# 1/rms of the feed-forward blocks as a row from a matrix of ones, in place of a column that is transposed

## The chip, the core and the metric

The kernel runs on one core of a Trainium2 chip. The metric is the time of one execution on the device in microseconds (us). TensorE is PE (its weight loads are PEld), VectorE is DVE, ScalarE is ACT, GpSimd is POOL, and SP is the engine that starts the loads. A matrix product takes its stationary operand (the weights) and a moving operand, and writes to PSUM, which POOL cannot read.

## What is computed

The reference is a decoder trunk of two layers on 256 tokens of 1024 features. Only the outline matters here:

```
for l in range(DEPTH):                       # DEPTH = 2
    x = x + 0.5 * _swiglu(_rmsnorm(x, ffn1_norm[l]), ffn1_w_gate[l], ffn1_w_up[l], ffn1_w_down[l])
    h = _rmsnorm(x, mix_norm[l])
    ...                                      # attention of three kinds on h @ w_in[l], then w_out[l]
    x = x + 0.5 * _swiglu(_rmsnorm(x, ffn2_norm[l]), ffn2_w_gate[l], ffn2_w_up[l], ffn2_w_down[l])
return _rmsnorm(x, final_norm)

def _rmsnorm(x, g):
    y = x32 * lax.rsqrt(jnp.mean(x32 * x32, axis=-1, keepdims=True) + RMS_EPS)
    return (y * g).astype(x.dtype)
def _swiglu(x, w_gate, w_up, w_down):
    return (jax.nn.silu(x @ w_gate) * (x @ w_up)) @ w_down
```

There are four feed-forward blocks (1024 to 2816 and back), two in each layer, with the attention between them.

## The kernel before

**Layout.** x is held transposed: `x[k]` has 128 features on the partitions and the 256 tokens on the free axis, for k from 0 to 7. The sum of squares of a token therefore runs over partitions. 1/rms of a token is needed as a *row*: the same 256 numbers on every partition (`rrow`), which is multiplied to the product x·W after the fact.

**Precision.** Every weight chunk (128x1024 numbers, `raw`) is split into a high part (`whi`, ACT, L157) and the rest (`wlo`, DVE, L158). The splits run three chunks ahead of PE (`SPLIT_AHEAD`). The operands `xx` hold x in the same two parts. `mm2` multiplies `whi` with both parts of x (512 columns) and `wlo` with the high part (256 columns); this pair of matmuls is the unit of PE's work.

**A feed-forward block** (`ffn`). `products(i, h)` runs eight pairs with one weight chunk; chunks (i, 0) and (i, 1) fill two PSUM banks, gate and up, of the column tile i, for i from 0 to 21. The banks come from two rings of four, and tile i+3 or so takes the banks of tile i. Behind them, for each i: `a` (DVE, L304, twice, with a copy `b` by ACT) adds the halves and frees the bank, `t` (DVE, L346) multiplies gate by the row, `s` (ACT) is silu, `sr` (POOL, L350) multiplies by the row again, `h` (DVE, L352) multiplies by up, and two more operations split h. Then the eight column tiles of the down projection follow.

**1/rms before.** The squares are summed over k on ACT and POOL (`ss`, `fold`). In products(2, 0), after the first pair (n = 0), `column` multiplies the sums by a column of ones: two matmuls with one moving column each (`pss`, L267 reads them) give mean squares with tokens on the partitions, as 128x2. DVE scales them (`ms`, L267), POOL raises them to the power -1/2 (`rcol`, L269). After pair n = 9, PE transposes the broadcast column (`prow`, L218) and DVE copies it out of PSUM (`rrow`, L281). The attention uses the same functions at other places, and `rcol` itself as well.

**What sets the order.** The engines' queues are in order; the scheduler of the framework places the instructions from the order of the code and its own estimates. PE's order is written down (`in_order`). The splits are put behind the instruction in `urgent`.

Of the kernel before, what the change touches and what calls it, by code (L numbers as in the profile page):

```python
# [10 lines left out]
F32 = mybir.dt.float32  # L11
F32R = mybir.dt.float32r
AF = mybir.ActivationFunctionType
OP = mybir.AluOpType

P = 128
D = 1024
T = 256
# [11 lines left out]
EPS = 1e-6  # L30
# [6 lines left out]
CH = DK * P  # L37
RAW, SPLIT_AHEAD = 5, 3
WARM = 12
AT = (0, 9)  # L40

FIRST = ((0, 1), (1, 4))

# [35 lines left out]
def tile_trunk(ctx, tc, xT, gains, kvg, sinks, table, onehot, wgu, wdn, winv, wins, wkv, wout, out):  # L79
    nc = tc.nc  # L80

    const = ctx.enter_context(tc.tile_pool(name="const", bufs=1))
    wpool = ctx.enter_context(tc.tile_pool(name="wpool", bufs=2))
    act = ctx.enter_context(tc.tile_pool(name="act", bufs=1))
    tmp = ctx.enter_context(tc.tile_pool(name="tmp", bufs=3))
# [3 lines left out]
    def bank(name, tag="mm"):  # L89
        return psum.tile([P, 512], F32, tag=tag, name=name)  # L90

    def f(ap):
        return ap.bitcast(F32)
# [33 lines left out]
    urgent = [None, None]  # L127
# [16 lines left out]
    def split(n, pieces=1, after=None):  # L144

        if n < len(chunks) and n not in parts:
            load(n)
            w = chunks[n][2]
            parts[n] = halves_of(n)
            step = w // pieces  # L150
            for c in range(0, w, step):
                split_part(n, c, c + step, after)
# [14 lines left out]
    def next_w(pieces=1, ahead=True):  # L167
        n = cursor[0]
        cursor[0] += 1
        split(n)  # L170
        if ahead:
            split(n + SPLIT_AHEAD, pieces)
        load(n + 2 * RAW - 1)
        return parts.pop(n)
# [23 lines left out]
                            fill=1.0, base=0, channel_multiplier=1)  # L198
    ones = const.tile([P, 1], F32, name="ones")
    nc.vector.memset(ones, 1.0)  # L200
    mhalf = const.tile([P, 2], F32, name="mhalf")
    nc.vector.memset(mhalf, -0.5)

# [7 lines left out]
    def in_order(ins):  # L211
        last_pe[0] = behind(ins, last_pe[0])

    def matmul(*a, **kw):
        in_order(nc.tensor.matmul(*a, **kw))  # L215

    def transpose(*a):
        in_order(nc.tensor.transpose(*a))  # L218
# [41 lines left out]
    def rms_column(sums, n):  # L260
# [8 lines left out]
        nc.gpsimd.tensor_tensor(out=col, in0=v, in1=mhalf, op=OP.pow)  # L269
        return col  # L270

    def rms_psum(col):

        p = bank("prow", "at")
        for b in range(2):
            transpose(p[:, b * P:(b + 1) * P], col[:, b:b + 1].to_broadcast([P, P]), ident)
        return p[:, :T]

    def rms_row(col):
        row = tmp.tile([P, T], F32, tag="rrow", name="rrow", bufs=2)  # L280
        urgent[1] = nc.vector.tensor_copy(row, rms_psum(col))  # L281
        return row
# [6 lines left out]
    def mm2(out, whi, wlo, both, first, last):  # L289

        matmul(out, whi, both.rearrange("p a t -> p (a t)"), start=first, stop=False)
        matmul(out[:, :T], wlo, both[:, 0, :], start=False, stop=last)

    def residual(a, b, p, scale, nxt, last=False):
        nc.vector.scalar_tensor_tensor(xs[:, a:b, :], p, scale, xs[:, a:b, :], op0=OP.mult, op1=OP.add)
        if not last:
            for k in range(a, b):
                nxt.operands(k)

    def add_halves(p, tag):  # L300
        b = tmp.tile([P, T], F32, tag=tag, name="b")
        nc.scalar.copy(b, p[:, T:])  # L302
        a = tmp.tile([P, T], F32, tag=tag, name="a")
        nc.vector.tensor_add(a, p[:, :T], b)  # L304
        return a

    def ffn(norm, nxt, last=False, first=None, between=(), at=AT):
        hs, banks, ws = [], {}, {}

        def products(i, h, start=0, stop=DK):  # L310

            if start == 0:
                ws[0] = next_w(ahead=(i, h) not in ((1, 1), (2, 0)))
                if h == 0:
                    for m in range(2):
                        banks[i, m] = bank("pgu", "at" if i % 3 == 2 else "mm")
            whi, wlo = ws[0]
            for j in range(start, stop):
                k, m = h * DK // 2 + j // 2, j % 2
                c = slice(j * P, (j + 1) * P)  # L320
                mm2(banks[i, m], whi[:, c], wlo[:, c], xx[k], k == 0, k == DK - 1)


        products(0, 0)
        products(0, 1)
        if first:
            first()
        products(1, 0)
        products(1, 1)
        for n in range(2 * DK):  # L330
            products(2, n // DK, n % DK, n % DK + 1)
            if n == at[0]:
                col = norm.column()
                for m in range(2):
                    split(cursor[0] + SPLIT_AHEAD - 2 + m)
            if n == at[1]:
                row = rms_row(col)
        for i in range(FK):
            if i in between:
                between[i]()  # L340
            if i > 2:
                products(i, 0)
                products(i, 1)
            g, u = add_halves(banks.pop((i, 0)), "A"), add_halves(banks.pop((i, 1)), "C")
            t = tmp.tile([P, T], F32, tag="A", name="t")
            nc.vector.tensor_mul(t, g, row)  # L346
            s = tmp.tile([P, T], F32, tag="B", name="s")
            nc.scalar.activation(s, t, AF.Silu)  # L348
            sr = tmp.tile([P, T], F32, tag="B", name="sr")
            nc.gpsimd.tensor_mul(sr, s, row)  # L350
            h = tmp.tile([P, T], F32, tag="h", name="h", bufs=2)
            nc.vector.tensor_mul(h, sr, u)  # L352
            hs.append(act.tile([P, 2, T], F32R, tag=("hh", "hl")[i % 2], name=f"h{i}", bufs=FK // 2))
            nc.scalar.copy(hs[i][:, 0, :], h)  # L354
            nc.vector.tensor_sub(hs[i][:, 1, :], h, f(hs[i][:, 0, :]))
        for k in range(DK):
            p = bank("pdn")
            for kk in range(FK):
                j = (k * FK + kk) % DK
                if j == 0:  # L360
                    whi, wlo = next_w()
                c = slice(j * P, (j + 1) * P)
                mm2(p, whi[:, c], wlo[:, c], hs[kk], kk == 0, kk == FK - 1)
            if last and k:
                turn(k - 1)
            nc.vector.scalar_tensor_tensor(x[k], p[:, T:], 0.5, x[k], op0=OP.mult, op1=OP.add)
            residual(k, k + 1, p[:, None, :T], 0.5, nxt, last)
            nxt.square(k, last)
            if last:
                ys[k] = tmp.tile([P, T], F32, tag="A", name="y")  # L370
                nc.scalar.activation(ys[k], x[k], AF.Copy, scale=nxt.g(k))
# [3 lines left out]
    def turn(k):  # L375

        for b in range(2):
            if k % 4 == 0:
                turned[b, k // 4] = bank("turned", ("mm", "at")[b])
            transpose(turned[b, k // 4][:, k % 4 * P:(k % 4 + 1) * P], ys[k][:, b * P:(b + 1) * P], ident)  # L380
# [334 lines left out]
    norm = Norm(0)  # L715
# [8 lines left out]
    start = norm  # L724
# [5 lines left out]
    for l in range(DEPTH):  # L730
        nxt = Norm(3 * l + 1)
        ffn(norm, nxt, first=first_squares if l == 0 else None, between={3: load_bias, 6: make_bias} if l == 0 else {})
        norm, nxt = nxt, Norm(3 * l + 2)
        mix(l, norm, nxt)
        norm, nxt = nxt, Norm(3 * l + 3)
        ffn(norm, nxt, last=l == DEPTH - 1)
        norm = nxt

    col = norm.column()
# [88 lines left out]
```

## Time and profile before

| | |
|---|---|
| median of three runs | 972.0 us (971.95 to 972.46) |
| the profiled execution | 966.4 us, span 964.6 us from the first to the last instruction |
| granted TensorE clock, mean over the span | 0.997 |
| busy: PE, DVE, ACT, POOL | 948.2, 689.9, 554.3, 180.7 us |
| pow on POOL (`rcol`), nine times | 10.0 us |

Busy time says how long an engine had an instruction in work. The durations below are from the profiled execution, whose own time is 5.6 us under the median of the runs.

### The profile page before, as it was taken

The numbers are of one execution on the slowest core, as the hardware profiler recorded it, in microseconds if no ns is written. First come the engines' busy times: TensorE is split into PE (matmuls) and PEld (weight loads), VectorE is DVE, ScalarE is ACT, GpSimd is POOL, SyncE is SP. The second block draws the span as 40 slices with busy tenths as digits, with TensorE's granted clock in tenths as the row PEclk, the third lists the DMA queues.
The fourth block names the chain that finished last, engine by engine and source line by source line (L and its number), as shares of the span: only waits on it lengthen the run. The fifth ranks groups of instructions, "written<-read, shape, count | busy, mean of one in ns | idle before, by whom it ended". The sixth has DMA issues, their size and how long they took to land.

```text
span 964.6 us, 15601 instructions
## 1 busy us (share of the span) xinstructions
PE 948.2 (98%) x5924; PEld 842.7 (87%) x5924; DVE 689.9 (72%) x1235; ACT 554.3 (57%) x1024; POOL 180.7 (19%) x156
## 2 busy tenths in 40 slices
PE   7999999999999999999999999999999999999996
PEld 6888888898899888888888888889988988888885
DVE  5787775659747888776668778666795578877552
ACT  6655554446875655554456555544487576655442
POOL 3221110121213212210022212001132042121001
PEclk9999999999999999999999999999999999999998
DMA  9688655554424565555555555555433345556511
GB/s 338 209 302 303 207 179 186 186 179 137 149 89 162 189 207 186 181 207 180 184 196 189 179 203 187 181 185 186 148 133 130 133 175 202 192 179 201 190 44 43
DMA packets 47575, 174.41 MB, mean 181 GB/s; under 512 B 3291, under 2 KB 5867, under 8 KB 47372
## 3 DMA queue, kind: packets, MB, share of 16 engines
q1 hardware_dynamic: 47212, 172.90, 51.4%
q8 instruction: 46, 0.75, 0.3%
q10 hardware_dynamic: 288, 0.52, 0.1%
q14 instruction: 29, 0.24, 0.1%
HBM read 172.34 MB, written 4.22 MB: 183 GB/s over the span
## 4 chain that ended last, share of the span: by engine, by line
PE 86%; DVE 4%; ACT 4%; issue 3%; POOL 1%; DMA 1%; SPq 0%; POOLq 0%; DVEq 0%; ACTq 0%
PE pgu L215 50%; PE pdn L215 22%; PE pwo L215 5%; PE pp L215 4%; PE pv L215 2%; ACT e L594 1%; ACT e L576 1%; DVE wlo L158 1%; POOL ss L248 1%; DVE acc L499 1%; PE po L215 1%; DVE m L498 1%; ACT whi L157 1%; DMA xs<-xT 1%; PE pt L218 1%
## 5 line engine op out<-in xcount | busy, mean ns | idle before, releaser
L215 PE MATMUL pgu<-xx,whi 128*128 128x512 f32 x1408 | 491.1, 393 | 2.4 <-DVE xx L235 1.5
L158 DVE TENSOR_TENSOR wlo<-raw,whi 128x1024 fp32r<-128x1024 f32 (+3 forms) x314 | 383.4, 1224 | 136.5 <-ACT whi L157 129.0
L157 ACT CAST whi<-raw 128x1024 fp32r<-128x1024 f32 (+2 forms) x322 | 332.7, 1034 | 244.1 <-PE pdn L215 108.1
L215 PE MATMUL pgu<-xx,wlo 128*128 128x256 f32 x1408 | 393.9, 280 | 0.2 <-DVE wlo L158 0.2
L215 PEld LDWEIGHTS pgu<-xx,whi 128*128 128x128 f32 x1408 | 263.6, 187 | 62.2 <-ACT whi L157 3.0
L215 PEld LDWEIGHTS pgu<-xx,wlo 128*128 128x128 f32 x1408 | 265.8, 189 | 0.9 <-DVE wlo L158 0.8
L215 PE MATMUL pdn<-h,whi 128*128 128x512 f32 x704 | 245.7, 394 | 0.0
L215 PE MATMUL pdn<-h,wlo 128*128 128x256 f32 x704 | 196.7, 279 | 0.0
L350 POOL TENSOR_TENSOR sr<-s,rrow 128x256 f32<-128x256 f32 x88 | 98.1, 1114 | 351.9 <-ACT s L348 351.6
L215 PEld LDWEIGHTS pdn<-h,whi 128*128 128x128 f32 x704 | 131.8, 187 | 29.6
L215 PEld LDWEIGHTS pdn<-h,wlo 128*128 128x128 f32 x704 | 132.9, 189 | 0.0
L302 ACT COPY b<-pgu 128x256 f32<-128x256 f32 x176 | 65.1, 371 | 78.8 <-PE pgu L215 78.8
L215 PE MATMUL pp<-xx,whi 128*128 128x256 f32 x480 | 90.7, 289 | 0.0
L304 DVE TENSOR_TENSOR a<-pgu,b 128x256 f32<-128x256 f32 x176 | 73.5, 419 | 23.6 <-ACT b L302 23.1
L215 PEld LDWEIGHTS pp<-xx,whi 128*128 128x128 f32 x480 | 74.2, 191 | 2.7 <-issue 1.7
L215 PE MATMUL pp<-xx,wlo 128*128 128x256 f32 x240 | 67.7, 282 | 0.0
L352 DVE TENSOR_TENSOR h<-sr,a 128x256 f32<-128x256 f32 x88 | 37.4, 425 | 29.1 <-POOL sr L350 28.7
L215 PE MATMUL pwo<-ohl,whi 128*128 128x256 f32 x256 | 47.6, 287 | 0.0
L248 POOL TENSOR_TENSOR ss<-sq 128x512 f32<-128x512 f32 x7 | 10.2, 1460 | 195.4 <-ACT sq L243 195.4
L354 ACT CAST h<-h 128x256 fp32r<-128x256 f32 x88 | 35.2, 400 | 19.0 <-DVE h L352 19.0
L215 PEld LDWEIGHTS pp<-xx,wlo 128*128 128x128 f32 x240 | 45.8, 191 | 0.0
L348 ACT ACTIVATE s<-t 128x256 f32<-128x256 f32 x88 | 37.4, 425 | 6.0 <-DVE t L346 5.5
(99 smaller groups left out, 714.4 us busy)
## 6 DMA issues: line engine op xcount, KB each, us to landing
raw<-wgu SPq DMA_DIRECT2D x86, 1024.0 KB, 5.0
raw<-wdn SPq DMA_DIRECT2D x44, 1024.0 KB, 5.0
raw<-wins SPq DMA_DIRECT2D x14, 1024.0 KB, 5.0
raw<-wout SPq DMA_DIRECT2D x8, 1024.0 KB, 4.9
raw<-winv SPq DMA_DIRECT2D x4, 776.0 KB, 4.3
w<-u SPq DMA_DIRECT2D x1, 3072.0 KB, 14.1
bias<-w SPq DMA_DIRECT2D x1, 2048.0 KB, 9.3
raw<-wgu SPq DMA_DIRECT2D x3, 512.0 KB, 8.1
```

The lines of the kernel that those rows point to most:

```text
L157: ops = (nc.scalar.copy(hi[:, a:b], raw(n, a, b)), low.tensor_sub(lo[:, a:b], raw(n, a, b), f(hi[:, a:b])))
L158: low.tensor_sub(lo[:, a:b], raw(n, a, b), f(hi[:, a:b])))
L215: in_order(nc.tensor.matmul(*a, **kw))
L218: in_order(nc.tensor.transpose(*a))
L248: nc.gpsimd.tensor_add(s, self.sums[0], sq)
L302: nc.scalar.copy(b, p[:, T:])
L304: nc.vector.tensor_add(a, p[:, :T], b)
L348: nc.scalar.activation(s, t, AF.Silu)
L350: nc.gpsimd.tensor_mul(sr, s, row)
L352: nc.vector.tensor_mul(h, sr, u)
L354: nc.scalar.copy(hs[i][:, 0, :], h)
L498: nc.vector.max(out=m8, in_=acc[:, cs])
```

## The change

In the four feed-forward blocks the sums of squares are multiplied by a 128x128 matrix of ones (`every`), which gives the sum of each token on every partition at once (`pss`, now 128x256). DVE scales it (`mrow`) and POOL raises all of it to -1/2 (`rrow`). The transposition after pair 9 and its copy are gone. The attention and the last norm keep the column.

```diff
-AT = (0, 9)
+AT = 0
...
+    every = const.tile([P, P], F32, name="every")
+    nc.vector.memset(every, 1.0)
...
+    def rms_spread(sums, n):
+
+        p = bank("pss", "at")
+        for i, s in enumerate(sums):
+            matmul(p[:, :T], every, s, start=i == 0, stop=i == len(sums) - 1)
+        v = tmp.tile([P, T], F32, tag="B", name="mrow")
+        urgent[1] = nc.vector.tensor_scalar(v, p[:, :T], 1.0 / n, EPS, op0=OP.mult, op1=OP.add)
+        row = tmp.tile([P, T], F32, tag="rrow", name="rrow", bufs=2)
+        nc.gpsimd.tensor_tensor(out=row, in0=v, in1=mhalf[:, 0:1].to_broadcast([P, T]), op=OP.pow)
+        return row
...
-            if n == at[0]:
-                col = norm.column()
+            if n == at:
+                row = rms_spread(norm.sums, D)
                 for m in range(2):
                     split(cursor[0] + SPLIT_AHEAD - 2 + m)
-            if n == at[1]:
-                row = rms_row(col)
```

On POOL, in each feed-forward block, the row of the power stands between the sum of squares and the 22 products `sr`. Before, in the second block of layer 0:

```order
L248 TENSOR_TENSOR ss<-sq 128x512
L248 TENSOR_TENSOR ss<-ss,sq 128x512 x2
L252 TENSOR_TENSOR fold<-ss 128x256
L269 TENSOR_TENSOR rcol<-ms,mhalf 128x2
L350 TENSOR_TENSOR sr<-s,rrow 128x256 x22
```

and now (the lines have moved by 2 to 13):

```order
L250 TENSOR_TENSOR ss<-sq 128x512
L250 TENSOR_TENSOR ss<-ss,sq 128x512 x2
L254 TENSOR_TENSOR fold<-ss 128x256
L282 TENSOR_TENSOR rrow<-mrow,mhalf 128x256
L361 TENSOR_TENSOR sr<-s,rrow 128x256 x22
```

Only the size of the power has changed there: 256 columns in place of 2. On DVE, the same block from the scaling of the mean squares on; the three `wlo` are the low parts of chunks (3, 0), (3, 1) and (4, 0), the first two `t` are those of the column tiles 0 and 1. Before:

```order
L267 TENSOR_SCALAR ms<-pss 128x2
L158 TENSOR_TENSOR wlo_3561<-raw_3345,whi_3560 128x1024
L158 TENSOR_TENSOR wlo_3565<-raw_3345,whi_3564 128x1024
L304 TENSOR_TENSOR a<-pgu,b 128x256
L281 COPY rrow<-prow 128x256
L158 TENSOR_TENSOR wlo_3583<-raw_3405,whi_3582 128x1024
L346 TENSOR_TENSOR t<-a,rrow 128x256
L304 TENSOR_TENSOR a<-pgu,b 128x256
L346 TENSOR_TENSOR t<-a,rrow 128x256
L158 TENSOR_TENSOR wlo_3667<-raw_3405,whi_3666 128x1024
```

and now:

```order
L280 TENSOR_SCALAR mrow<-pss 128x256
L158 TENSOR_TENSOR wlo_3556<-raw_3341,whi_3555 128x1024
L158 TENSOR_TENSOR wlo_3560<-raw_3341,whi_3559 128x1024
L357 TENSOR_TENSOR t<-a,rrow 128x256
L317 TENSOR_TENSOR a<-pgu,b 128x256
L158 TENSOR_TENSOR wlo_3578<-raw_3401,whi_3577 128x1024
L317 TENSOR_TENSOR a<-pgu,b 128x256
L363 TENSOR_TENSOR h<-sr,a 128x256
L357 TENSOR_TENSOR t<-a,rrow 128x256
L317 TENSOR_TENSOR a<-pgu,b 128x256
```

The copy is gone, and the first `t`, which reads the row, has moved ahead of the `a` of tile 1 and of the split of chunk (4, 0). The other three blocks read alike around `mrow`.

## Rows read from the trace of the kernel before

**Rows 1.** The page, part 1: busy us (share of the span) xinstructions of each engine.

```profile
PE 948.2 (98%) x5924; PEld 842.7 (87%) x5924; DVE 689.9 (72%) x1235; ACT 554.3 (57%) x1024; POOL 180.7 (19%) x156
```

**Rows 2.** Waits of PE over the span: who for whom, total us, times, longest.

```profile
PE pss L215 <- ACT sq L511: 1.8, 2, 1.0
...
PE pss L215 <- POOL fold L252: 1.2, 1, 1.2
...
PE pgu L215 <- DVE wlo L158: 0.2, 1, 0.2
```

**Rows 3.** Timeline of PE, second block of layer 0: start, us, engine, line, operation.

```profile
310.69 0.60 PE L215 MATMUL pss<-ones,fold 128*128 128x1 f32 x4
311.16 0.48 PE L215 MATMUL pgu<-xx,whi 128*128 128x512 f32 x1
...
314.42 0.38 PE L218 MATMUL prow<-ident,rcol 128*128 128x128 f32 x2
314.56 0.48 PE L215 MATMUL pgu<-xx,whi 128*128 128x512 f32 x1
...
316.74 0.39 PE L215 MATMUL pgu<-xx,whi 128*128 128x512 f32 x1
...
319.51 0.39 PE L215 MATMUL pgu<-xx,whi 128*128 128x512 f32 x1
319.74 0.28 PE L215 MATMUL pgu<-xx,wlo 128*128 128x256 f32 x1
...
322.28 0.39 PE L215 MATMUL pgu<-xx,whi 128*128 128x512 f32 x1
```

**Rows 4.** Timeline of POOL, the same block; in brackets the idle time before.

```profile
311.58 1.63 POOL L269 TENSOR_TENSOR rcol<-ms,mhalf 128x2 f32<-128x2 f32 x1 [0.94 <-DVE ms L267]
319.68 1.80 POOL L350 TENSOR_TENSOR sr<-s,rrow 128x256 f32<-128x256 f32 x2 [6.47 <-ACT s L348]
```

**Rows 5.** Timeline of DVE, the same block.

```profile
311.34 0.16 DVE L267 TENSOR_SCALAR ms<-pss 128x2 f32<-128x2 f32 x1 [0.63 <-PE pss L215]
311.42 2.36 DVE L158 TENSOR_TENSOR wlo<-raw,whi 128x1024 fp32r<-128x1024 f32 x2
313.69 0.42 DVE L304 TENSOR_TENSOR a<-pgu,b 128x256 f32<-128x256 f32 x1
314.84 0.42 DVE L281 COPY rrow<-prow 128x256 f32<-128x256 f32 x1 [0.73 <-PE prow L218]
315.18 1.22 DVE L158 TENSOR_TENSOR wlo<-raw,whi 128x1024 fp32r<-128x1024 f32 x1
316.31 0.42 DVE L346 TENSOR_TENSOR t<-a,rrow 128x256 f32<-128x256 f32 x1
```

**Rows 6.** The tile rcol: POOL's power, duration ns min/median/max, first and last start.

```profile
L269 POOL TENSOR_TENSOR rcol<-ms,mhalf x9: 699/705/1631, 23.6 to 957.9; 128x2 f32<-128x2 f32 x9
```

**Rows 7.** The tile rrow: POOL's product by the row, same columns.

```profile
L350 POOL TENSOR_TENSOR sr<-s,rrow x88: 737/1126/1557, 31.8 to 893.7; 128x256 f32<-128x256 f32 x88
```

**Rows 8.** The tile ss: POOL's sum of squares, same columns.

```profile
L248 POOL TENSOR_TENSOR ss<-sq x7: 1297/1357/1797, 14.7 to 924.6; 128x512 f32<-128x512 f32 x7
```

**Rows 9.** Timeline of all engines in the first block, POOL beside DVE.

```profile
18.80 2.24 POOL L248 TENSOR_TENSOR ss<-ss,sq 128x512 f32<-128x512 f32 x1
...
20.12 2.00 DVE L158 TENSOR_TENSOR wlo<-raw,whi 128x1024 fp32r<-128x1024 f32 x1
```

**Rows 10.** Timeline of PE in the attention: a full-precision product of 256 columns, two passes.

```profile
258.82 0.68 PE L215 MATMUL pk<-cg,wk 128*128 128x256 f32 x2
259.34 0.55 PE L215 MATMUL pk<-wk,cg 128*128 128x64 f32 x4
```

**Rows 11.** Stretches at the end: us, busy of PE, PEld, DVE, ACT, POOL, granted clock, DMA.

```profile
950.00:958.00 8.00, 6.81 (x44) 5.83 (x42) 1.01 (x3) 1.03 (x2) 0.11 (x1) 1.00 0.00 0
958.00:964.60 6.60, 0.00 (x0) 0.00 (x0) 1.41 (x2) 1.26 (x2) 0.59 (x1) 0.50 0.42 159
```

**Rows 12.** Timeline of ACT, second block of layer 0.

```profile
319.19 0.42 ACT L348 ACTIVATE s<-t 128x256 f32<-128x256 f32 x1
```

## The prediction

> **What bounds the kernel now.** I read the shares of busy time first, then what PE waited for, then the second block of layer 0 engine by engine. PE is busy for 948.2 of 964.6 us [rows 1], and its eight kinds of wait add up to 9.5 us, from 1.8 to 0.2 [rows 2]. So PE is the bound: whatever the change moves on DVE or POOL gains nothing, unless PE comes to wait for it, and then all of that wait is paid.
>
> What has to be seen in the block is how much time lies between the mean squares and the first need of what hangs on them. PE goes on at 311.16, behind `pss`, with 15 more pairs of products(2), starts products(3, 0) at 316.74 and (3, 1) at 319.51, where the first matmul with the low part stands at 319.74, and products(4, 0) at 322.28 [rows 3]; a pair takes 0.35 us. DVE has `ms` at 311.34, then the low parts of chunks (3, 0) and (3, 1), 2.36 us for both, and is through with them at 313.78 [rows 5]. So chunk (3, 1) is ready 6 us early. The power on POOL starts at 311.58 and ends at 313.21 [rows 4], and the longest of PE's waits in all, 1.8 us, is for something else [rows 2].
>
> **PE's part of the change.** Removed are the `pss` of one column, 311.16 - 310.69 = 0.47 us, and the transpositions, 314.56 - 314.42 = 0.14 us [rows 3]. Added is one full-precision product with 256 moving columns; the nearest row is `pk`, of that very shape, which takes 259.34 - 258.82 = 0.52 us [rows 10]. Together -0.1 us for each block. The wait for `fold` ahead of `pss`, 1.2 us in one block [rows 2], stays, since the place of `pss` does.
>
> **DVE's part.** `ms` (0.16 us) and the copy (0.42 us) go [rows 5]; `mrow` has 256 columns from PSUM as the copy has, so 0.42 us at the same place. Bounds: 0.16 to 0.42. DVE is 72% busy [rows 1], and the 0.2 us less are behind PE's work. The memset of the matrix of ones, once, lies ahead of all loads. These edits cost nothing as long as DVE keeps its lead. No transfer is added or moved.
>
> **The power.** This is the term that decides. The row of before shows it with 2 columns only: 699 ns at least, 705 in the median, up to 1631 [rows 6]. The long ones are those in the feed-forward blocks: the power starts at 311.58, just after a split has started on DVE at 311.42, and ends 0.6 us after that split is over (half of 2.36 us, at 312.60) [rows 4, 5]. So a split and a POOL instruction hold each other up. It goes the other way too: a split that takes 1.22 us alone [rows 5] takes 2.00 us at 20.12, when a sum on POOL runs until 21.04, and ends 1.08 us after it [rows 9].
>
> What do 256 columns cost? Two bounds:
> - From below, by the shape: a product of 256 columns takes 737 ns at least [rows 7], a sum of 512 columns 1297 [rows 8]. That is 2.2 ns for a column and 177 ns for an instruction. If the power cost 2.2 ns for a column, and the rest of its 700 ns were paid once, it would take 1.3 us.
> - From above, by the operation: of the 700 ns, 177 are those of any instruction, which leaves 523 ns for 2 columns, 261 ns for each. By that, 256 columns take 0.18 + 256 x 0.261 = 67 us. If even the 177 ns were paid by the column, 256 x 0.35 = 90 us.
>
> A rule of the Trainium skill speaks for the lower end: its page GPSIMD Engine Reference, section Performance versus the Vector engine, gives about 2.6 cycles an element for a two-input operation, measured with an add; at its clock of 1.2 GHz that is an estimate of 0.55 us for 256 columns, and by it the change would cost nothing (971.6 us, first rival). The sum and the product in this trace agree, 2.2 ns a column; the power of 2 columns, at 700 ns in place of some 181, does not.
>
> I take the upper row, 261 ns a column, because it is the only one of this operation, and the product and the sum differ from it in kind, not only in size: it spends 519 ns more than the product's line gives for 2 columns. How much of this is paid once, no row says.
>
> **What is late, then.** `mrow` ends at some 311.9 (0.26 us more than `ms`, and a longer `pss`), the first split follows and ends at about 313.0; the power then reads, and ends 0.61 us later if it has 2 columns. So the row is there at R = 313.6 + 254 c, where c is the price of a column. The second split stands behind the first on DVE and, by what the rows show of splits and POOL, waits for the power; it ends at R + 1.2. PE needs it at 319.74 - 0.14 + 0.05, about 319.65. Nothing else PE could do is ahead of it. So PE waits R + 1.2 - 319.65 us, if that is above zero: from c = 19 ns on. With c = 261 ns, R = 380.0 and PE waits 61.6 us. Should the split slip in ahead of the power, the next in line is products(4), due at 322.1: the second bank of it is freed by the `a` that stands behind the first `h`, and this behind `t`, `s` and `sr`, 2.5 to 3 us after R (0.42 + 0.42 + 0.74 to 1.13 + 0.42 + 0.42) [rows 5, 7, 12]; PE would wait 60 to 61 us all the same.
>
> Behind the wait two things are to be paid. DVE has the work of two column tiles to make good, and chunk (4, 1) stands behind six operations of 256 columns (0.42 us each) and its own split of 1.22 us [rows 5], 3.7 us in all, against 2.8 us of PE's next eight pairs: about 1 us. And PE's clock: at the end, PE runs nothing from 958.0 on, and the granted clock is 0.50, half of 2.4 GHz, where it was 1.00 [rows 11]. A wait of 60 us will end at the half clock. No row shows for how long; bounds 0 to 4 us lost, I take 1.5. Together 2.5 us.
>
> **The sum.** For each block 61.6 + 2.5 - 0.1 = 64.0 us; the four blocks are built alike, so 256 us. The profiled execution's own time is 966.4 us (span 964.6), which makes 1222; the median of the runs is 5.6 us above it, and so is my forecast: 1228 us.
>
> **The rivals.**
> 1. *The power is hidden: not slower.* POOL pays its 519 ns once and then 2 to 19 ns a column. With 2.2 ns, R = 314.2, the second split ends at 315.4, 4 us ahead of PE. What is left is 4 x -0.1 = -0.4 us: 971.6 us. For it: the lines of sum and product [rows 7, 8]. Against it: the 700 ns for two columns [rows 6]. It decides below 19 ns a column; above, each 10 ns cost 4 x 2.54 = 10 us. A gain above 0.2% (2 us, about what a measurement of this kernel can tell from no change) could only come from order, since 9.5 us of waits is all that PE has [rows 2].
> 2. *POOL overlaps its columns.* Two columns may be too few to show a rate: a loop that has four in work would pay 261 / 4 = 65 ns for each. Then R = 330.1, PE waits 11.7 us, and 14.1 us a block give 972.0 + 56 = 1028 us. The Trainium skill, GPSIMD Engine Reference, section Performance pitfalls for Q7 kernels, says that a chain of dependent fp32 steps costs 4 cycles a step, and that unrolling into at least four independent ones hides it; whether the power is unrolled no run here shows. For it: nothing in the rows contradicts it. Against it: the product gives the rate at once.
> 3. *Costlier still:* 350 ns a column, 972.0 + 4 x 86.7 = 1319 us, if nothing is paid once. Against it: the 177 ns that each POOL instruction shows.
>
> **How the numbers follow.** Forecast (150 to 290 ns a column, 1115 to 1257 us): 0.48. Overlapped (19 to 150 ns, 972 to 1115 us): 0.34. Hidden: 0.15, of which 0.12 within 0.2% and 0.03 faster. Above 290 ns: 0.03. The range leaves out the hidden case, the first few us of the overlapped one and the costliest: 985 to 1250 us. Faster 0.03, same 0.12, slower 0.85.
>
> **What would show it.** Right: four instructions `rrow<-mrow,mhalf` on POOL of some 67 us each; a split on DVE that ends just behind each; PE waiting for `wlo` some 62 us four times, at the second chunk of the column tile 3; granted clock 0.5 in these waits. `pss` at 0.5 us and no `prow` in these blocks. Wrong: a power of 1 to 5 us with no wait behind it (first rival), or 5 to 40 us (second). The forecast fails most easily in the price of a column, which is taken from two of them.

## The result: 1117.7 us, and the profile after

The median went from 972.0 us (971.2 to 972.5, four runs) to 1117.7 us (1114.9 to 1119.0, four runs). The ratio is 1.150, interval 1.147 to 1.153. That is 145.7 us more, 36.4 for each of the four blocks. The profiled execution of after takes 1119.0 us (span 1117.2), which is 152.6 more than that of before, because that one lay 5.6 us under its median and this one lies 1.3 over. Three executions that lie far above all others (3974.4 us of the kernel before, 1163.6 and 1332.6 us of the experiment e9) are left out of the medians and ranges below.

The page of after, parts 1, 2 (two rows: the granted clock, and PE's busy tenths in 40 slices of 28 us) and 5 (the power's group: busy, mean ns, idle before and for whom):

```profile
PE 968.0 (87%) x5908; PEld 851.3 (76%) x5908; DVE 690.9 (62%) x1232; ACT 554.1 (50%) x1024; POOL 343.6 (31%) x156
...
PE   8259999999999089999970999999999943999997
...
PEclk9669999999999589999995899999999985999999
...
L282 POOL TENSOR_TENSOR rrow<-mrow,mhalf 128x256 f32<-128x256 f32 x4 | 168.2, 42051 | 12.0 <-DVE mrow L280 12.0
```

Against [rows 1]: POOL has 162.9 us more work; the four powers take 168.2 us, where the long ones of [rows 6] took 1.63 us each. In PE's row there are four holes, and the granted clock is down in each. PE is busy for 19.8 us longer with 16 matmuls less: that is pace, in part the pairs at the lower clock that the timeline below shows.

The waits of the whole span, for all engines and then for PE alone (who for whom, total us, times, longest):

```profile
ACT s L359 <- DVE t L357: 163.6, 24, 39.7
DVE t L357 <- POOL rrow L282: 157.9, 4, 39.5
PEld pgu L217 <- ACT s L359: 131.9, 4, 33.1
PE pgu L217 <- ACT s L359: 130.7, 4, 32.8
...
PE pgu L217 <- DVE a L317: 1.6, 2, 0.8
...
PE pgu L217 <- DVE wlo L158: 1.3, 5, 0.3
```

Read it from below: PE waits 130.7 us, four times some 32.7, put down to `s` on ACT; `s` waits for `t` on DVE; `t` waits for the power. The wait for `wlo`, which the prediction named, is 1.3 us in all, and most of it is for another chunk than the prediction's, (4, 0).

The second block of layer 0, engine by engine (timeline: start, us, instruction, idle before it). POOL:

```profile
351.38 42.06 POOL L282 TENSOR_TENSOR rrow<-mrow,mhalf 128x256 f32<-128x256 f32 x1 [1.30 <-DVE mrow L280]
```

DVE:

```profile
350.87 0.42 DVE L280 TENSOR_SCALAR mrow<-pss 128x256 f32<-128x256 f32 x1 [0.73 <-PE pss L217]
351.21 2.77 DVE L158 TENSOR_TENSOR wlo<-raw,whi 128x1024 fp32r<-128x1024 f32 x2
393.47 0.42 DVE L357 TENSOR_TENSOR t<-a,rrow 128x256 f32<-128x256 f32 x1 [39.48 <-POOL rrow L282]
393.81 0.42 DVE L317 TENSOR_TENSOR a<-pgu,b 128x256 f32<-128x256 f32 x1
394.14 1.21 DVE L158 TENSOR_TENSOR wlo<-raw,whi 128x1024 fp32r<-128x1024 f32 x1
395.28 0.41 DVE L317 TENSOR_TENSOR a<-pgu,b 128x256 f32<-128x256 f32 x1
```

ACT:

```profile
393.93 0.42 ACT L359 ACTIVATE s<-t 128x256 f32<-128x256 f32 x1 [38.35 <-DVE t L357]
394.25 0.63 ACT L315 COPY b<-pgu 128x256 f32<-128x256 f32 x2
```

PE:

```profile
350.13 0.70 PE L217 MATMUL pss<-fold,every 128*128 128x256 f32 x2
350.48 0.58 PE L217 MATMUL pgu<-xx,whi 128*128 128x512 f32 x1
...
361.50 0.28 PE L217 MATMUL pgu<-xx,wlo 128*128 128x256 f32 x1
394.38 0.77 PE L217 MATMUL pgu<-xx,whi 128*128 128x512 f32 x1 [32.59 <-ACT s L359]
395.41 0.58 PE L217 MATMUL pgu<-xx,wlo 128*128 128x256 f32 x1 [0.27 <-DVE wlo L158]
395.79 0.75 PE L217 MATMUL pgu<-xx,whi 128*128 128x512 f32 x1
396.55 0.63 PE L217 MATMUL pgu<-xx,whi 128*128 128x512 f32 x1
...
399.05 0.40 PE L217 MATMUL pgu<-xx,whi 128*128 128x512 f32 x1
399.41 0.39 PE L217 MATMUL pgu<-xx,whi 128*128 128x512 f32 x1
```

The two splits behind `mrow` are both through at 353.98, 2.77 us where [rows 5] have 2.36: neither waited for the power. So PE had chunk (3, 1) in time and went on to the end of column tile 3, at 361.78. There it stopped for the two banks of products(4, 0), which the column tile 1 still holds. The first is freed by the `a` at 393.81, which stands on DVE behind the first `t`; the second by the `a` at 395.28, whose copy `b` (394.25) stands on ACT behind the first `s`. Both engines are in order, so both stood still behind one operand, the row. The split of chunk (4, 0), at 394.14, stands behind the same `t` and `a`, so PE would have been held there too, one matmul later; after the wait it costs 0.27 us more (395.41). The power ends at 393.44 and PE starts 0.94 us later. Of what it waits for, the view names the one that came last, `s`, through at 394.35; that `a` was through at 394.23. For the reading it makes no difference, as both stand behind `t`. PE then runs at the lower pace, 0.64 us for a pair, until 399.05, and at 0.35 from there.

### The profile page after: what moved, and what is told of

It is laid out like the page before. It is cut to its first block, busy times and chain, and to the rows that moved or that the text cites. A ratio compares the mean times of both kernels' runs of the same rounds, so it can differ in the third digit from the quotient of the medians.

```text
span 1117.2 us, 15577 instructions
## 1 busy us (share of the span) xinstructions
PE 968.0 (87%) x5908; PEld 851.3 (76%) x5908; DVE 690.9 (62%) x1232; ACT 554.1 (50%) x1024; POOL 343.6 (31%) x156
## 4 chain that ended last, share of the span: by engine, by line
PE 72%; POOL 16%; DVE 4%; ACT 3%; issue 3%; DMA 1%; SPq 0%; POOLq 0%; DVEq 0%; ACTq 0%
PE pgu L217 40%; PE pdn L217 19%; POOL rrow L282 15%; PE pwo L217 4%; PE pp L217 4%; PE pv L217 2%; DVE wlo L158 1%; ACT e L605 1%; ACT e L587 1%; POOL ss L250 1%; DVE acc L510 1%; PE po L217 1%; DVE m L509 1%; ACT whi L157 1%; DMA xs<-xT 1%
## 5 line engine op out<-in xcount | busy, mean ns | idle before, releaser
L217 PE MATMUL pgu<-xx,whi 128*128 128x512 f32 x1408 | 506.5, 403 | 134.2 <-ACT s L359 130.7
L158 DVE TENSOR_TENSOR wlo<-raw,whi 128x1024 fp32r<-128x1024 f32 (+3 forms) x314 | 385.1, 1228 | 137.8 <-ACT whi L157 130.5
L217 PEld LDWEIGHTS pgu<-xx,whi 128*128 128x128 f32 x1408 | 268.6, 191 | 201.6 <-ACT s L359 131.9
L217 PE MATMUL pgu<-xx,wlo 128*128 128x256 f32 x1408 | 399.7, 284 | 1.3 <-DVE wlo L158 1.3
L217 PEld LDWEIGHTS pgu<-xx,wlo 128*128 128x128 f32 x1408 | 270.5, 192 | 4.0 <-DVE wlo L158 3.9
L282 POOL TENSOR_TENSOR rrow<-mrow,mhalf 128x256 f32<-128x256 f32 x4 | 168.2, 42051 | 12.0 <-DVE mrow L280 12.0
L357 DVE TENSOR_TENSOR t<-a,rrow 128x256 f32<-128x256 f32 x88 | 37.4, 425 | 160.6 <-POOL rrow L282 157.9
L250 POOL TENSOR_TENSOR ss<-ss,sq 128x512 f32<-128x512 f32 x13 | 21.1, 1623 | 102.7 <-ACT sq L245 76.8
```

Of the source, the lines that this page charges most:

```text
L158: low.tensor_sub(lo[:, a:b], raw(n, a, b), f(hi[:, a:b])))
L250: nc.gpsimd.tensor_add(s, self.sums[0], sq)
L282: nc.gpsimd.tensor_tensor(out=row, in0=v, in1=mhalf[:, 0:1].to_broadcast([P, T]), op=OP.pow)
```

## The experiments

The theory from this profile: each column of the power costs about 0.16 us, PE can run for some 9 us on what lies ahead of the row, and pays all the rest, with a few us behind it. The rivals: that it is the matrix, or the new order, that costs time; that POOL holds DVE for the whole power, as the prediction had it; and that most of the loss behind the wait is the clock.

**e1_product: the same row and order with a cheap operation.** The row is the constant 0.3 here, and 1/rms isn't computed in the four blocks.

```diff
-        urgent[1] = nc.vector.tensor_scalar(v, p[:, :T], 1.0 / n, EPS, op0=OP.mult, op1=OP.add)
+        urgent[1] = nc.vector.tensor_scalar(v, p[:, :T], 1e-9, -0.6, op0=OP.mult, op1=OP.add)
...
-        nc.gpsimd.tensor_tensor(out=row, in0=v, in1=mhalf[:, 0:1].to_broadcast([P, T]), op=OP.pow)
+        nc.gpsimd.tensor_tensor(out=row, in0=v, in1=mhalf[:, 0:1].to_broadcast([P, T]), op=OP.mult)
```

> The change with POOL's power made a product, at the same place, of the same shape and with the same broadcast operand; the mean square ahead of it is replaced by a constant (the product then gives 0.3 for every token), so that the blocks work without their norm. If the price lies in the power itself, the POOL instruction takes 0.74 us alone and 1.3 to 1.7 us beside a split, PE has no wait in column tile 4, and the time is that of before less 0.4 us: 971 to 972 us. Rival: the price lies in the broadcast second operand or in the row as such; then the instruction takes 42 us again and the time stays at 1118 us. Second rival: the new order on DVE (the first t ahead of tile 1's sums) costs by itself; then 974 us or more.

973.1 us (970.0 to 973.7), ratio 1.004, interval 1.002 to 1.005; 971 to 972 was expected. The tile `mrow` (ns min/median/max, first and last start):

```profile
L282 POOL TENSOR_TENSOR rrow<-mrow,mhalf x4: 1522/1524/1527, 23.8 to 786.6; 128x256 f32<-128x256 f32 x4
```

With 256 columns of a product in place of the power, all four waits of 32.7 us are gone, and the loss with them but for 4 us (973.1 against 968.8 for the kernel before, measured beside it). So the operation is the cause, not the order and not the size as such. The 4 us are taken up below.

**e2_128_columns and e3_32_columns: less of the power.** The first 128 (or 32) columns are raised on POOL; the rest of the row is set to 0.3 by one more operation on DVE, so 1/rms is computed for these tokens only. The diff with 128:

```diff
-        urgent[1] = nc.vector.tensor_scalar(v, p[:, :T], 1.0 / n, EPS, op0=OP.mult, op1=OP.add)
...
-        nc.gpsimd.tensor_tensor(out=row, in0=v, in1=mhalf[:, 0:1].to_broadcast([P, T]), op=OP.pow)
+        nc.vector.tensor_scalar(row[:, 128:], p[:, 128:T], 1e-9, 0.3, op0=OP.mult, op1=OP.add)
+        urgent[1] = nc.vector.tensor_scalar(v[:, :128], p[:, :128], 1.0 / n, EPS, op0=OP.mult, op1=OP.add)
+        nc.gpsimd.tensor_tensor(out=row[:, :128], in0=v[:, :128], in1=mhalf[:, 0:1].to_broadcast([P, 128]), op=OP.pow)
```

> The change with the power taken of 128 of the 256 columns; the other half of the row is set to 0.3, by one more DVE instruction. Theory: the price is 0.38 us for an instruction, some 0.159 us a column, and 0.93 us where it starts beside a split (from 0.70 and 1.63 us for 2 columns and 42.05 us for 256). By that 21.7 us for 128 columns, 20.4 us less wait in each block, 1118 - 82 = 1036 us. Rival: the price of a column as I forecast it, 0.261 us, and a limit that caps the long one at 42 us: 34 us, 1086 us. Rival: the price is one of the instruction, whatever its size above some few columns: 42 us, 1118 us.

> As with 128 columns, but the power is taken of 32 columns, the rest of the row is 0.3. Theory: 0.38 + 32 x 0.159 + 0.93 = 6.4 us. The row is then there some 36 us earlier than with 256, which is more than the 32.7 us that PE waits: no wait is left, or some tenths of a us for the second bank of tile 4, and no fall of the clock: 972 to 975 us. Rival: what PE pays behind the wait (5 us a block) comes from the new order on DVE and not from the wait: 985 to 992 us.

With 128 columns 1035.5 us, ratio 1.069 (1.065 to 1.072); with 32 columns 973.2 us, ratio 1.003 (1.002 to 1.005). The power with 128 columns (tile `mrow`):

```profile
L283 POOL TENSOR_TENSOR rrow<-mrow,mhalf x4: 21637/21654/21658, 23.8 to 835.5; 128x128 f32<-128x128 f32 x4
```

PE's wait with 128 columns (waits of PE):

```profile
PE pgu L217 <- ACT s L360: 49.4, 4, 12.4
```

The power with 32 columns (tile `mrow`):

```profile
L283 POOL TENSOR_TENSOR rrow<-mrow,mhalf x4: 6335/6339/6347, 24.2 to 786.7; 128x32 f32<-128x32 f32 x4
```

With 2, 32, 128 and 256 columns the power beside a split takes 1.63 [rows 4], 6.34, 21.65 and 42.05 us. The three steps are 157, 159 and 159 ns a column: a straight line. And PE's wait is the power less some 9.3 us, 21.65 - 12.35 and 42.05 - 32.7; with 6.34 us there is none. That is the cover, and the timeline has it too: from the start of the power, 351.38, PE has work until 361.78, which is 10.4 us, less the 0.94 us from the row to its restart: 9.5 us in this block. With 128 columns the loss is 66.8 us against the kernel before beside it, 49.4 of them waits: so 4.4 us a block come on top of a wait of 12.4 us, and with 256 columns 3.7 on top of one of 32.7, the same within what executions of one kernel differ by (some 1 us a block).

**e4_power_beside: a long power with nothing waiting for it.** In the kernel before, a power of 256 columns is started on POOL behind the last `sr` of each block; no one reads its result.

```diff
+            last_sr = nc.gpsimd.tensor_mul(sr, s, row)
...
+        spare = tmp.tile([P, T], F32, tag="spare", name="spare", bufs=1)
+        behind(nc.gpsimd.tensor_tensor(out=spare, in0=row, in1=mhalf[:, 0:1].to_broadcast([P, T]), op=OP.pow), last_sr)
```

> The kernel before, with one more power of 128x256 on POOL in each feed-forward block, behind the last product by the row; nothing reads its result, and it runs while the down projection does. Forecast's picture, that a split on DVE waits until a POOL instruction is over: a split of 40 us in each block, PE out of weights after three chunks (8 us), some 33 us lost a block, 1100 us or more. Rival: the power holds a split only while it reads or writes, which is little of its time: the splits stay at 1.2 to 1.5 us, and the time is that of before, 971 to 974 us.

968.6 us, ratio 1.001 (0.999 to 1.002). POOL and DVE in the first block (timeline):

```profile
140.32 41.13 POOL L357 TENSOR_TENSOR spare<-rrow,mhalf 128x256 f32<-128x256 f32 x1
```

```profile
144.16 1.22 DVE L158 TENSOR_TENSOR wlo<-raw,whi 128x1024 fp32r<-128x1024 f32 x1 [1.32 <-ACT whi L157]
...
146.97 1.23 DVE L158 TENSOR_TENSOR wlo<-raw,whi 128x1024 fp32r<-128x1024 f32 x1 [0.79 <-ACT whi L157]
```

Four powers of 41.1 us cost nothing when nobody waits for them, and the splits beside them take 1.21 to 1.23 us, as alone [rows 5]. So POOL does not hold DVE for the length of a power. A power that starts with no split in work takes 41.12 us, 0.93 less than one that starts just behind a split; with two columns it is 1.63 against 0.70 [rows 4, 6], the same 0.93.

**e7_pe_kept_busy and e8_pe_busy_longer: the clock behind the wait.** To the changed kernel 130 (150) matmuls are added ahead of column tile 4, whose results are unread; they fill the wait, so that PE doesn't stand still.

```diff
+            if i == 4:
+                busy = bank("busy", "at")
+                for _ in range(130):
+                    matmul(busy, xx[0][:, 0, :P], xx[0].rearrange("p a t -> p (a t)"), start=True, stop=True)
```

> The change as it is, with 130 matmuls of 512 columns, whose result nothing reads, between products(3) and products(4) of each block: they fill about 30 of the 32.7 us that PE waits there. Theory: of the 5 us that a block loses behind the wait, some 2.5 to 3 us are pairs at half the clock (0.64 us each in place of 0.35, for eight or nine pairs); with PE busy the granted clock stays at 1.00 and the time falls by 10 to 12 us, to 1106. Rival: DVE's arrears set the pace behind the wait and the clock is hidden by them: 1118 us, as without.

> The change as it is with 150 matmuls in the wait in place of 130, 0.228 us each by the run with 130: 34.2 us, so that PE is busy from products(3) until about 1 us before the second bank of column tile 4 is free. The clock should now stay at 1.00. Theory that the half clock costs time behind the wait: the pairs behind it take 0.35 us from the first on, and a block gains what eight pairs lose at half the clock, 2.3 us, less about 1 us for which DVE's split of chunk (4, 1) is then late: 4 x 1.3 to 4 x 2.3 us, 1107 to 1113 us where the change has 1115 to 1118. Rival: DVE's arrears alone set the pace: as the change.

The 130 were too few, and that run is inconclusive: they end 3.3 us ahead of the bank, two gaps of 0.6 and 0.8 us follow, and the clock falls all the same. 1115.9 us, ratio 1.152 (1.150 to 1.154). With 150 it stays up: 1115.0 us (1114.4 to 1116.3), ratio 1.148 (1.145 to 1.150), mean clock 0.997. Two stretches of the first block with 130 (us, busy of PE, PEld, DVE, ACT, POOL, granted clock, DMA):

```profile
64.00:70.00 6.00, 1.77 (x4) 1.09 (x5) 3.39 (x8) 1.75 (x6) 3.38 (x2) 0.80 0.00 0
70.00:76.00 6.00, 6.00 (x25) 5.15 (x24) 5.58 (x12) 4.64 (x9) 1.81 (x2) 0.63 0.27 90
```

The second of them with 150:

```profile
70.00:76.00 6.00, 5.19 (x30) 4.26 (x29) 5.58 (x11) 4.64 (x9) 1.81 (x2) 1.00 0.29 94
```

PE there, with 150 (timeline):

```profile
69.19 0.50 PE L217 MATMUL pgu<-xx,whi 128*128 128x512 f32 x1 [0.82 <-DVE a L317]
...
71.76 0.40 PE L217 MATMUL pgu<-xx,whi 128*128 128x512 f32 x1
72.96 0.39 PE L217 MATMUL pgu<-xx,wlo 128*128 128x256 f32 x1 [0.81 <-DVE wlo L158]
73.19 0.39 PE L217 MATMUL pgu<-xx,whi 128*128 128x512 f32 x1
```

And PE in the same place of the changed kernel (timeline):

```profile
66.75 0.77 PE L217 MATMUL pgu<-xx,whi 128*128 128x512 f32 x1 [32.58 <-ACT s L359]
...
69.17 0.79 PE L217 MATMUL pgu<-xx,whi 128*128 128x512 f32 x1 [0.80 <-DVE a L317]
69.97 0.63 PE L217 MATMUL pgu<-xx,whi 128*128 128x512 f32 x1
...
74.45 0.51 PE L217 MATMUL pgu<-xx,whi 128*128 128x512 f32 x1
```

In both, the second pair starts at 69.2, when DVE has freed its bank. From there a pair takes 0.35 us at the full clock and 0.64 at the half one, but the faster PE then runs into the split of chunk (4, 1) and waits 0.8 us for it. The tenth pair starts at 73.19 and at 74.45. So the half clock costs 1.3 us in this block. In the four blocks the tenth pair starts 7.37, 5.19, 7.39 and 5.42 us behind the row with 150, and 8.64, 6.66, 8.53 and 7.19 us behind it in the changed kernel: 1.3, 1.5, 1.1 and 1.8 us, 1.4 in the mean. (The 150 run on until 2.2 to 2.4 us behind the row, so the first pair is 1.1 to 1.3 us late. The second pair is not, but for 0.2 us in the last block.) Not all of this reaches the end: the spans differ by 4.1 us and the medians by 2.8, and further on PE waits 0.3 us for `whi` in two of the blocks, where the changed kernel doesn't. The medians alone would not show the clock's part: 1107 to 1113 us was expected if the clock counts, 1115.0 was measured, and the single runs of the two kernels overlap (1114.4 to 1116.3 and 1114.9 to 1119.0).

**e5_matrix_alone, e6_no_matrix, e9_matrix_unread: the rest of 0.4%.** In e1 and e3 nothing waits, and yet they lie 0.3 to 0.4% over before. Is it the matrix? e5 is the kernel before with the matrix set up and unread. e6 is e1 without it; the stationary operand of `pss` is the column of ones, broadcast. e9 is e6 with the matrix set up but unread. In e6 and e9 the row is 0.3, as in e1.

```diff
-            matmul(p[:, :T], every, s, start=i == 0, stop=i == len(sums) - 1)
+            matmul(p[:, :T], ones.to_broadcast([P, P]), s, start=i == 0, stop=i == len(sums) - 1)
```

> The kernel before with the matrix of ones (128x128, 512 bytes of each partition) set up and never used; all tiles behind it lie 512 bytes further on. The product in place of the power was 0.37% slower than before, some 3.6 us, with no wait to show for it. Theory: the pace of PE's pairs depends on where the tiles lie; then this kernel loses about the same, 1.002 to 1.005 of before. Rival: the loss comes from the new order on DVE and POOL in the blocks; then this is before, 0.999 to 1.001.

> The product in place of the power, as in the first experiment, but with the matrix of ones read from the column of ones that is there already, by a step of zero: no new tile, all else as there. Theory that the place of the tiles counts: back at before, 0.999 to 1.001. Rival, the new order on DVE and POOL: 1.003 to 1.004 as with the tile.

> The product in place of the power; the matrix of ones is set up, so that all tiles lie where they lie in the first experiment, but the matmul reads the column of ones by a step of zero, as in the sixth. Theory that the place of the tiles makes PE's pairs slower, together with the new order: 1.003 to 1.005 of before. Rival: what counts is that PE loads the matrix itself: 0.999 to 1.001.

e5: 968.6 us, ratio 1.000 (0.999 to 1.001). e6: 967.5 us, ratio 1.000 (0.998 to 1.002). e9: 969.5 us, ratio 0.998 (0.996 to 1.000). So the matrix set up and unread costs nothing, and without reading it the 0.4% did not show.

**e10_product_again, e11_no_matrix_again, e12_before_itself: is that a difference at all?** e1, e6 and the kernel before are run again, as they were, side by side.

> The first experiment once more, the product in place of the power with the matrix of ones, beside its form without the matrix and beside before itself. If the 0.37% of the first experiment belongs to this program, 1.0025 to 1.005 again; if it belongs to how a program happened to lie on that chip, anywhere from 0.997 to 1.004.

> The sixth experiment once more, the product without the matrix: 0.999 to 1.001 if the difference belongs to the programs, anywhere from 0.997 to 1.004 if not.

> The kernel before, unchanged, treated as a changed one. Its ratio to before says what difference this measurement can show where there is none: 0.999 to 1.001 if the interval is to be trusted for loads of the same program, up to 0.003 off if not.

e1 again: 972.9 us, ratio 1.001 (0.999 to 1.003). e6 again: 967.1 us, ratio 0.996 (0.994 to 0.997). Before against itself: 972.0 us, 1.001 (0.999 to 1.003). e1's ratio has moved by 0.24% and e6's by 0.43%, with nothing changed in them. Nearly all of that is the kernel before: its median was 968.8 and 968.9 beside the first e1 and e6 and 971.1 here, while those of e1 and e6 moved by 0.2 and 0.4 us. Its single runs go from 965.8 to 974.8. The traces show what such a step is made of. The kernel before from 60 to 100 us, in the profiled execution of before (span 964.6 us) and in that of e12 (span 973.0 us), which is the same kernel (stretches, columns as under e7):

```profile
60.00:100.00 40.00, 40.00 (x233) 34.95 (x232) 31.94 (x51) 23.13 (x43) 8.64 (x8) 1.00 0.84 302
```

```profile
60.00:100.00 40.00, 40.00 (x228) 34.71 (x228) 31.19 (x50) 22.87 (x42) 8.15 (x8) 1.00 0.85 302
```

PE is busy throughout, at the full clock, and gets through 233 matmuls in one execution and 228 in the other: a pair takes 0.347 or 0.353 us. Whole stretches run at one pace or the other. Over the 2074 pairs whose starts follow each other by 0.3 to 0.4 us the mean is 347.5 and 351.5 ns, which is the 8.4 us between the two spans. In the profiled execution of e1 it is 351.5 ns, in that of e10, the same kernel, 349.7. So the 0.4% is PE's pace and not a wait. What sets the pace of a stretch no run here shows. e6 was below e1 both times, by 0.4 and 0.6%; whether reading the matrix makes the slower stretches more frequent, some 4 us in all, stays open. It is at most a fortieth of the change.

## Why the prediction held, and where it was off

1228 us was forecast and 1117.7 measured: the side, the block and the kind of loss were right, its size was not, 256 us where 146 were measured. Of the signs that it named, the clock of 0.50 in the waits and the missing `prow` came. The power of 67 us, a split that ends just behind it and the wait for `wlo` did not, and at 42 us the power is just above the 5 to 40 us that it named as a sign of being wrong.

**The step that failed is the price of a column**: "of the 700 ns, 177 are those of any instruction, which leaves 523 ns for 2 columns, 261 ns for each". Measured: 700 ns with 2 columns and 41.12 us with 256 (e4), which is 40.42 / 254 = 159 ns a column, and 0.38 us paid once. The once-paid part of the power is twice that of a sum or a product, and with 2 columns the error of 0.2 us in it became 102 ns a column. The other rows had shown how POOL's simpler operations start, not how this one does. The prediction said that no row told how much was paid once, and that it would fail most easily here. 159 ns lies inside the band of its likeliest case, 150 to 290, near the lower edge.

**R, the time of the row, was right as a formula.** With 159 ns it gives 354.0, 42.7 us after `ms`; measured, the row stands 393.44 - 350.87 = 42.6 us after `mrow` starts. With it the same working gives a wait of 35.5 us and 972 + 4 x 37.9 = 1124 us, 6 more than measured.

**What PE waits for was wrong.** "The second split ... waits for the power": it did not, and e4 shows that a power of 41 us holds no split. The short additions on POOL do hold one [rows 9], and I had carried that over to a power of any length. The page SBUF — State Buffer of the Trainium skill, section SBUF: two separate sides, has the same rule: a DVE operation with two SBUF inputs and a GpSimd operation share a port pair, and whoever starts first has it for the whole instruction. By that rule the split at 144.16 would have ended behind 181.45; it took 1.22 us, and the measurement decides. The prediction's fallback, products(4) waiting for banks behind `t`, `s` and `a`, was the true path, but it looked at the second bank alone. The first is what PE stops for: it is needed at 322.28 in the times of before [rows 3], 2.6 us after the split would be, and PE restarts 0.94 us behind the row, not 1.2. So the wait is 32.7 us, not 35.5, and by an estimate from these prices there is none below some 50 columns ((9.3 - 0.93 - 0.38) / 0.159). The second bank comes 2.25 us behind the row in the block shown and 3.3 in the first, where its `a` stands behind `h`, as was foreseen with 2.5 to 3.

**Behind the wait** 2.5 us were set down, 1 for DVE's arrears and 1.5 for the clock. From the first pair behind the wait to the tenth, PE takes 7.70, 5.72, 7.59 and 6.25 us in the four blocks, where nine pairs at 0.35 would take 3.15: 3.7 us lost in the mean. By e8 the clock's part of it is 1.4, close to the 1.5 set down; the arrears are the larger part, 2.3 and not 1. The prediction had left out of them the second bank, for which PE waits another 0.8 us in two of the blocks, and the low part of chunk (4, 0), for which it waits 0.27 us in each.

**PE's part** is small, as forecast. `pss` takes 350.48 - 350.13 = 0.35 us and the pair behind it 0.54 in place of 0.35, 0.54 in all. Before, `pss` took 0.47 us [rows 3] and the transpositions 0.14, and the prediction left out that the pairs behind them, too, took 0.08 and 0.09 us more than others. Together that is -0.2 us and not -0.1. DVE's part is hidden, as forecast: `mrow` takes 0.42 us.

**The sum, as measured**: 4 x (32.7 + 3.7 - 0.2) = 144.8 us, of the 145.7 between the medians. That is closer than PE's pace lets one tell, which moves whole executions by several us.

**The rivals.** Hidden: refuted for the power (42 us), and e1 and e3 show its other side. With 1.5 or 6.3 us on POOL the kernel runs at 973 us, within 0.4% of before, so there is such a condition. Its limit of 19 ns a column was worked out from the split; by the bank it is some 30 ns ((9.3 - 1.63) / 254). The page GPSIMD Engine Reference of the Trainium skill, section Performance versus the Vector engine, gives 2.6 cycles an element for an addition; by an estimate from it 256 columns would take 0.55 us. The product's 0.74 us [rows 7] is near that, and the power's 41 us shows that it says nothing of this operation. Overlapped columns: with 32, 128 and 256 columns the rate does not fall, so nothing is gained by having more of them; 159 is above that rival's 65 ns and its upper bound of 150. Costlier (350 ns; its own working gives 1318 us, not 1319): refuted. No version here beats the kernel before by a margin that came twice: with a nearly free row, e1 and e6 gave from -0.4 to +0.4%, and PE has no wait there to win back.

## What to carry to other kernels

A price taken from an instruction with 2 columns can be mostly its once-paid part, here 0.38 of 0.70 us: run or find a second size before it is multiplied by 128. Do an operation that is dear by the column where it has few columns, here 1/rms as 128x2, and spread the result afterwards, even if that takes a transposition. Before work is made longer on an engine that is off the path, count how far the bound engine can run on what stands ahead of the first in-order wait (here 9.3 us); all that goes beyond is paid in full, and each wait cost some 4 us more behind it, the short one (12.4 us) as the long one (32.7 us). And read a difference of 0.4% against the same kernel's own scatter first.

## What the runs showed that I had not expected

How POOL and DVE hold each other up depends on the operation. An addition of 2.24 us on POOL stretched a split from 1.22 to 2.00 us [rows 9], but a power of 41.1 us let every split beside it run in 1.21 to 1.23 us (e4). A split that is in work when a power starts makes the power 0.93 us longer, with 2 columns as with 256. And PE's pairs have two paces at the full clock, 0.347 and 0.353 us (e12).

PE's clock did not fall with the wait, but within it, and did not rise with the first matmul. The changed kernel, first block (stretches, columns as above); PE's last matmul before the wait ends at 34.2 and the first one behind it starts at 66.75:

```profile
34.00:36.00 2.00, 0.17 (x2) 0.00 (x0) 0.00 (x0) 0.00 (x0) 2.00 (x1) 1.00 0.00 0
36.00:38.00 2.00, 0.00 (x0) 0.00 (x0) 0.00 (x0) 0.00 (x0) 2.00 (x1) 0.79 0.00 0
38.00:64.00 26.00, 0.00 (x0) 0.00 (x0) 0.00 (x0) 0.00 (x0) 26.00 (x1) 0.50 0.00 0
...
72.00:74.00 2.00, 2.00 (x8) 1.71 (x8) 2.00 (x3) 1.20 (x2) 1.08 (x1) 0.50 0.19 12
74.00:76.00 2.00, 2.00 (x12) 1.73 (x11) 1.98 (x5) 1.87 (x4) 0.00 (x0) 0.83 0.75 250
76.00:78.00 2.00, 2.00 (x14) 1.74 (x13) 1.89 (x3) 1.39 (x3) 0.91 (x1) 1.00 0.65 266
```

The granted clock is at 1.2 GHz (0.50) from the stretch behind 38 until past 74, with PE fully busy from 70 on; PE's pairs are back at full pace from 74.9, 8.2 us behind its first matmul. In the other blocks that is 4.7 (399.05), 7.6 and 5.9 us; the two shorter ones are those in which PE did not wait for the second bank. More than that the rows do not say about when the clock comes back.
